# The rotary part of the row maxima as pairs of 64-row products on the two halves of TensorE

## The chip, the cores and the metric

The kernel runs on one core of a Trainium2 chip. The metric is the device time of one execution in microseconds, as the median of several runs. A profile of one execution stands beside it: what each engine did, instruction by instruction. The engines are TensorE (PE in the profile, with its weight loads as PEld), VectorE (DVE), ScalarE (ACT), GpSimd (POOL) and SyncE (SP), which issues transfers.

## The reference

Two layers of a diffusion backbone over 1024 latent tokens and 256 context tokens, 1024 channels wide. Layer 0 is multi-head latent attention with eight heads, layer 1 a gated long convolution. The change lies in the attention of layer 0. A query and a key have a part of 128 channels that each head has for itself and a rotary part of 64 channels, of which the key's is shared by all heads:

```python
def scores(qn_, qr_, kn_, kr_):
    s = jnp.einsum('bqhd,bkhd->bhqk', qn_, kn_) + jnp.einsum('bqhr,bkr->bhqk', qr_, kr_)
    return s.astype(jnp.float32) * scale
...
s = jnp.concatenate([scores(qn_b, qr_b, kn, kr), scores(qn_b, qr_b, knc, krc)], axis=-1)
p = jax.nn.softmax(s, axis=-1).astype(v.dtype)
```

The latent queries read 1024 + 256 = 1280 keys.

## The kernel before, in words

Everything is float32. For exactness a value is split into a high part, rounded to the narrower fp32r, and the rest, also fp32r; `split` (L95) makes the first by a cast on ACT and the second by a subtraction on DVE. A product of two split values is three matmuls (`mm3`, L117, its matmuls on L119 to L121): high with high, high with low, low with high.

The program has three stages: the projections of layer 0 and the filters of layer 1 (to about 435 us in the profile), the attention (to about 910 us), and layer 1. In the attention the work is cut into 16 units, each one head and 512 queries (`units`). For each unit `attend` goes over ten blocks of 128 keys: five matmuls make the transposed scores S (three with the split keys `kn` and queries `qn`, one of `krh` with `r1` at L825, one of `krl` with `r2` at L826), ACT takes the exponential, ACT and DVE split it, DVE adds it to `acc`, and three matmuls add its product with the values to O. At the end of a unit DVE takes the reciprocal of the sums (L855).

The rotary parts lie in tiles made for these five matmuls. `krh` has the high part of the key's 64 channels twice, in rows 0 to 63 and again in 64 to 127. `r1` has the high part of the queries' 64 channels in one half and the low part in the other, so that one matmul over 128 rows gives the key's high part times both. `r2` has the high part in rows 0 to 63, for the key's low part in `krl`, and in row 64 the negative row maximum, which a row of ones in `krl` subtracts from the scores. `rope` makes `r1` and `r2` for two heads at a time (L745 to L751).

The row maxima are what `row_max` (L755) makes for the unit ahead. For each of four tiles of 128 queries and each of three key segments (512, 512 and 256 wide, `ksegs`) it takes one of the two buffers of the PSUM pool `apx`, puts into it the product of the high parts `qn[0]` and `kn[0]` (L762) and that of `r1` and `krh` (L763, over 128 rows), and DVE reduces it to its maximum (L764). That is 12 buffers a unit, 192 in all. Each maximum is moved by a matmul with an identity (L769) and negated into row 64 of `r2`. The maxima only shift the exponent and cancel in the softmax.

`row_max` is a generator that yields after each buffer. `advance` lets it go two steps for each block of the unit that is being attended to. A scheduler then puts each engine's instructions into one fixed order; engines run theirs in that order and wait for each other by semaphores. Elsewhere the kernel has other matmuls that use a part of TensorE's array: `packed` (L123 to L134, matmul at L128) puts four products on 32 columns each, for the modulation vectors and the sums of squares, and `rms_steps` transposes pieces of 128, 96 or 64 rows at L396.

Of the kernel before, what the change touches and what calls it, by code (L numbers as in the profile page):

```python
# [11 lines left out]
F32 = mybir.dt.float32  # L12
F32R = mybir.dt.float32r
AF = mybir.ActivationFunctionType
ALU = mybir.AluOpType
AX = mybir.AxisListType
# [3 lines left out]
P = 128  # L20
# [35 lines left out]
class Net:  # L56
# [627 lines left out]
    def attention(self):  # L684
        nc, a = self.nc, self.a
        v, act, mm = nc.vector, nc.scalar, nc.tensor.matmul
        ps = self.open("psA", 2, space=PSUM)
        bank = lambda: ps.tile([P, 512], F32, tag="pj", name="pj")
        px = self.open("psX", 2, space=PSUM)
        tp = self.open("attt", 2)  # L690
        ckv, krh, krl, cq, cos, sin = self.att
# [5 lines left out]
        ksegs = [(0, 512), (512, 512), (1024, 256)]  # L697
# [33 lines left out]
        def rope(wb, sl):  # L731
            b = bank()
            for k in range(KQ):
                c = slice(P * k, P * k + P)
                self.mm3(b, (wb[0][:, c], wb[1][:, c]), (cq[0][k][:, sl], cq[1][k][:, sl]), k == 0, k == KQ - 1)
            x, y, q = [tp.tile([P, 512], F32, tag=f"rp{i}", name="rp", bufs=1) for i in range(3)]
            act.copy(out=x, in_=b)
            for p in range(0, P, 32):
                nc.sync.dma_start(out=y[p ^ 32 : (p ^ 32) + 32], in_=x[p : p + 32])
            v.tensor_tensor(out=q, in0=x, in1=cos[:, sl], op=ALU.mult)  # L740
            yield
            v.tensor_tensor(out=y, in0=y, in1=sin[:, sl], op=ALU.mult)
            v.tensor_tensor(out=q, in0=q, in1=y, op=ALU.add)
            out = []
            for j in range(2):  # L745
                r1 = tp.tile([P, 512], F32R, tag="r1", name="r1", bufs=5)
                r2 = tp.tile([65, 512], F32R, tag="r2", name="r2", bufs=5)
                me, ot = slice(64 * j, 64 * j + 64), slice(64 - 64 * j, 128 - 64 * j)
                act.copy(out=r1[me], in_=q[me])
                v.tensor_tensor(out=r1[ot], in0=q[me], in1=r1[me], op=ALU.subtract)  # L750
                act.copy(out=r2[0:64], in_=r1[me])  # L751
                out.append((r1, r2))
            return out

        def row_max(kn, qn, r1, r2):  # L755
            cm = tp.tile([P, 4, 3], F32, tag="cm", name="cm")
            mx = tp.tile([P, 4], F32R, tag="mx", name="mx")
            for t in range(4):
                c = slice(P * t, P * t + P)
                for i, (o, w) in enumerate(ksegs):  # L760
                    b = px.tile([P, 512], F32, tag="apx", name="apx")
                    mm(b[:, :w], lhsT=qn[0][:, c], rhs=kn[0][:, o : o + w], start=True, stop=False)  # L762
                    mm(b[:, :w], lhsT=r1[:, c], rhs=krh[:, o : o + w], start=False, stop=True)  # L763
                    v.tensor_reduce(out=cm[:, t, i : i + 1], in_=b[:, :w], axis=AX.X, op=ALU.max)  # L764
                    yield
            v.tensor_reduce(out=mx, in_=cm, axis=AX.X, op=ALU.max)
            b = bank()
            for t in range(4):
                mm(b[0:1, P * t : P * t + P], lhsT=mx[:, t : t + 1], rhs=identr, start=True, stop=True)  # L769
            act.activation(out=r2[64:65], in_=b[0:1], func=AF.Copy, scale=-1.0)  # L770
# [6 lines left out]
        def ahead():  # L777

            for pr in range(HEADS // 2):
                wc = self.kvw if pr == 0 else self.load_kv_weights(pr)  # L780
                wq, wr = self.qw if pr == 0 else self.load_q_weights(pr)
                vals[pr] = (wc, [])
                rr = {}
                for j in range(2):
                    kn = yield from keys(wc, j)
                    for sl in halves:
                        if j == 0:
                            rr[sl.start] = yield from rope(wr, sl)
                        qn = queries(wq, j, sl)
                        yield  # L790
                        if not ready and pr == 0 and len(vals[0][1]) == 0:
                            vals[0][1].extend(value(wc, t) for t in range(10))
                        r1, r2 = rr[sl.start][j]
                        yield from row_max(kn, qn, r1, r2)
                        ready[pr, j, sl.start] = (kn, qn, r1, r2)
# [652 lines left out]
```

## Time and profile before

| What | Value |
|---|---|
| Median of three runs | 1736.26 us (1733.69 to 1740.81) |
| The profiled execution's own time | 1731.71 us |
| Span from its first to its last instruction | 1729.9 us |
| Mean granted clock of TensorE over the span | 0.979 |
| Span before the attention stage, of it and after it, roughly | 435, 475 and 820 us |
| Reductions of the row maxima on DVE | 192, from 446.9 to 908.9 us |

A line of a group in the profile reads: source line, engine, operation, tile written and tiles read, shapes, count, then the busy time in us and the mean of one in ns, then the idle time of the engine just before and what ended it. A line of the timeline reads: start, duration (both us), engine, source line, operation. For a matmul `64*128` means 64 contraction rows and 128 columns of the array. Matmuls are pipelined: each is shown from its start to the modelled end of its last result, so neighbours overlap, and the cost of one in a row of them is the distance between starts.

### The profile page before, as it was taken

How to read it: one execution, taken by the hardware profiler on the slowest of the kernel's cores; microseconds unless marked ns; L12 is line 12 of the kernel's file. 1: busy time of each engine (PE TensorE's matmuls, PEld its weight loads, DVE VectorE, ACT ScalarE, POOL GpSimd, SP SyncE). 2: the span in 40 equal slices, each digit the busy share in tenths (PEclk: the TensorE clock that was granted, in tenths of full speed). 3: DMA queues.
4: the chain of work that ended last, by engine and by line, in shares of the span. 5: the costliest groups of instructions: out<-in, count | busy, mean ns of one | idle time of the engine just before them, and what ended most of it. 6: DMA issues, size and time to landing. Idle time of an engine off the chain costs nothing.

```text
span 1729.9 us, 22940 instructions
## 1 busy us (share of the span) xinstructions
PE 1633.5 (94%) x8160; PEld 1299.5 (75%) x8160; DVE 1442.2 (83%) x2558; ACT 766.3 (44%) x1337; POOL 16.0 (1%) x43
## 2 busy tenths in 40 slices
PE   5899897899999999999999999999999999999996
PEld 2467676787788788788787777888888888887874
DVE  4886979895699899899899456999999999999856
ACT  4533444445455465555555345433433433343313
POOL 1000000000000000000000010000000000000000
PEclk9899999899999999999999999999999999999998
DMA  9777664436101001010014771332332332244545
GB/s 342 256 231 222 200 187 120 138 89 206 28 27 37 25 32 38 19 33 25 25 56 132 232 254 64 101 98 83 101 115 83 104 106 89 95 122 134 180 142 197
DMA packets 140759, 206.15 MB, mean 119 GB/s; under 512 B 13578, under 2 KB 71649, under 8 KB 140516
## 3 DMA queue, kind: packets, MB, share of 16 engines
q1 hardware_dynamic: 137508, 194.00, 35.7%
q0 software_dynamic: 3136, 10.69, 1.9%
q8 instruction: 64, 1.05, 0.3%
q14 instruction: 51, 0.42, 0.1%
HBM read 148.92 MB, written 53.61 MB: 117 GB/s over the span
## 4 chain that ended last, share of the span: by engine, by line
PE 75%; DVE 10%; DMA 9%; ACT 3%; issue 2%; SPq 1%; DVEq 0%; ACTq 0%
PE pj L121 12%; PE pj L119 12%; PE pj L120 12%; DMA dec<-in_dec 2%; PE O L120 2%; PE S L119 2%; PE O L119 2%; PE S L826 2%; PE O L121 2%; PE apx L762 2%; PE S L825 2%; PE S L121 2%; PE S L120 2%; PE apx L763 2%; PE fu L119 2%; PE fy L119 2%
## 5 line engine op out<-in xcount | busy, mean ns | idle before, releaser
L96 ACT CAST w<-wr 128x512 fp32r<-128x512 f32 (+1 forms) x149 | 90.7, 609 | 259.5 <-PE pj L120 129.5
L119 PE MATMUL pj<-a,w 128*128 128x512 f32 x512 | 203.1, 397 | 1.7 <-ACT a L422 1.6
L121 PE MATMUL pj<-a,w 128*128 128x512 f32 x512 | 203.1, 398 | 0.0
L120 PE MATMUL pj<-a,w 128*128 128x512 f32 x512 | 203.0, 397 | 0.0
L828 ACT ACTIVATE p<-S 128x512 f32<-128x512 f32 x160 | 95.7, 598 | 148.2 <-DVE acc L835 69.5
L97 DVE TENSOR_TENSOR w<-wr,w 128x512 fp32r<-128x512 f32 (+1 forms) x149 | 98.8, 671 | 54.7 <-ACT w L96 54.6
L96 ACT CAST bh<-raw 128x512 fp32r<-128x512 f32 x128 | 77.1, 620 | 89.1 <-DVE raw L1071 71.0
L119 PEld LDWEIGHTS pj<-a,w 128*128 128x128 f32 x512 | 96.4, 188 | 22.0 <-ACT a L422 2.4
L120 PEld LDWEIGHTS pj<-a,w 128*128 128x128 f32 x512 | 96.5, 188 | 19.9 <-DVE a L423 0.2
L121 PEld LDWEIGHTS pj<-a,w 128*128 128x128 f32 x512 | 96.6, 189 | 19.5 <-issue 0.8
L97 DVE TENSOR_TENSOR p<-p 128x512 fp32r<-128x512 f32 x160 | 109.4, 684 | 1.5 <-ACT p L96 1.2
L764 DVE TENSOR_REDUCE cm<-apx 128x1 f32<-128x512 f32 (+1 forms) x192 | 107.1, 591 | 3.8 <-PE apx L763 3.1
L835 DVE TENSOR_TENSOR acc<-acc,p 128x512 f32<-128x512 f32 x144 | 98.7, 685 | 7.6 <-ACT p L828 6.7
L121 PE MATMUL pj<-pg,w 128*128 128x512 f32 (+1 forms) x248 | 96.5, 389 | 8.7 <-DVE w L97 8.6
L96 ACT CAST p<-p 128x512 fp32r<-128x512 f32 x160 | 99.5, 622 | 4.8
L119 PE MATMUL pj<-pg,w 128*128 128x512 f32 (+1 forms) x248 | 95.7, 389 | 2.7 <-ACT pg L422 2.7
L120 PE MATMUL pj<-pg,w 128*128 128x512 f32 (+1 forms) x248 | 96.6, 389 | 0.6 <-DVE pg L423 0.6
L97 DVE TENSOR_TENSOR bl<-raw,bh 128x512 fp32r<-128x512 f32 x128 | 84.7, 686 | 9.1 <-ACT bh L96 9.0
L119 PE MATMUL u<-bh,fm 128*128 128x256 f32 (+1 forms) x200 | 68.2, 342 | 12.2 <-ACT bh L96 9.5
L762 PE MATMUL apx<-kn,qn 128*128 128x512 f32 (+1 forms) x192 | 69.0, 364 | 2.2 <-DVE cm L764 1.9
L321 DVE TENSOR_TENSOR kk<-ph,dec 128x512 f32<-128x512 f32 x64 | 42.6, 684 | 33.2 <-DMA dec<-in_dec 26.6
L763 PE MATMUL apx<-krh,r 128*128 128x512 f32 (+1 forms) x192 | 67.1, 357 | 0.0
(312 smaller groups left out, 4408.9 us busy)
## 6 DMA issues: line engine op xcount, KB each, us to landing
aw<-in_adaw SPq DMA_DIRECT2D x32, 512.0 KB
kd<-ko SPq DMA_DIRECT2D x128, 128.0 KB
wr<-in_hw SPq DMA_DIRECT2D x64, 256.0 KB
kt<-kd SPq DMA_DIRECT2D x56, 256.0 KB
wr<-in_w SPq DMA_DIRECT2D x34, 256.0 KB
dec<-in_dec SPq DMA_DIRECT2D x64, 128.0 KB
pg<-in_adaw SPq DMA_DIRECT2D x32, 256.0 KB
wr<-in_wo SPq DMA_DIRECT2D x32, 256.0 KB
```

Of the source, the lines that this page charges most:

```text
L96: self.nc.scalar.copy(out=hi, in_=raw)
L97: self.nc.vector.tensor_tensor(out=lo, in0=raw, in1=hi, op=ALU.subtract)
L119: mm(out, lhsT=w[0], rhs=x[0], start=start, stop=False)
L120: mm(out, lhsT=w[0], rhs=x[1], start=False, stop=False)
L121: self.last = mm(out, lhsT=w[1], rhs=x[0], start=False, stop=stop)
L321: nc.vector.tensor_tensor(out=kk, in0=ps, in1=dec.broadcast_to([P, 2, 2, P]), op=ALU.mult)
L762: mm(b[:, :w], lhsT=qn[0][:, c], rhs=kn[0][:, o : o + w], start=True, stop=False)
L763: mm(b[:, :w], lhsT=r1[:, c], rhs=krh[:, o : o + w], start=False, stop=True)
L764: v.tensor_reduce(out=cm[:, t, i : i + 1], in_=b[:, :w], axis=AX.X, op=ALU.max)
L825: mm(S, lhsT=krh[:, c], rhs=r1, start=False, stop=False)
L828: act.activation(out=p, in_=S, func=AF.Exp, scale=ASCALE)
L835: v.tensor_tensor(out=acc, in0=acc, in1=p, op=ALU.add)
```

## The change

The changed kernel takes the rotary product of a buffer with the queries' high part alone, which has 64 rows. Two buffers are taken together. The first has its rotary product on rows 0 to 63 of TensorE (the high part in `r2`, the first copy in `krh`), the second on rows 64 to 127 (the high part in `r1`, the second copy in `krh`), each with a tile position that names its half. The one on the upper rows is issued first, the other right behind it. The low part of the queries is left out of the maxima. The six pairs of a unit are the two 512-wide segments of each query tile, and the 256-wide segments of two query tiles; the products with `kn` stay one for each buffer, and so do the reductions, which now stand behind the pair. `rope` puts the high part for both heads into rows 64 to 127 of `r1`, with the same number of casts, subtractions and copies.

```diff
-                me, ot = slice(64 * j, 64 * j + 64), slice(64 - 64 * j, 128 - 64 * j)
-                act.copy(out=r1[me], in_=q[me])
-                v.tensor_tensor(out=r1[ot], in0=q[me], in1=r1[me], op=ALU.subtract)
-                act.copy(out=r2[0:64], in_=r1[me])
+                me = slice(64 * j, 64 * j + 64)
+                same = r2[0:64] if j == 0 else r1[64:128]
+                act.copy(out=same, in_=q[me])
+                v.tensor_tensor(out=r1[0:64], in0=q[me], in1=same, op=ALU.subtract)
+                act.copy(out=r1[64:128] if j == 0 else r2[0:64], in_=same)
...
-            for t in range(4):
-                c = slice(P * t, P * t + P)
-                for i, (o, w) in enumerate(ksegs):
-                    b = px.tile([P, 512], F32, tag="apx", name="apx")
-                    mm(b[:, :w], lhsT=qn[0][:, c], rhs=kn[0][:, o : o + w], start=True, stop=False)
-                    mm(b[:, :w], lhsT=r1[:, c], rhs=krh[:, o : o + w], start=False, stop=True)
-                    v.tensor_reduce(out=cm[:, t, i : i + 1], in_=b[:, :w], axis=AX.X, op=ALU.max)
-                    yield
+            for pair in (((0, 0), (0, 1)), ((0, 2), (1, 2)), ((1, 0), (1, 1)),
+                         ((2, 0), (2, 1)), ((2, 2), (3, 2)), ((3, 0), (3, 1))):
+                halves_ = []
+                for half, (t, i) in enumerate(pair):
+                    o, w = ksegs[i]
+                    c = slice(P * t, P * t + P)
+                    b = px.tile([P, 512], F32, tag="apx", name="apx")[:, :w]
+                    mm(b, lhsT=qn[0][:, c], rhs=kn[0][:, o : o + w], start=True, stop=False)
+                    rows, rq = slice(64 * half, 64 * half + 64), (r2, r1)[half]
+                    halves_.append((b, rq[rows, c], krh[rows, o : o + w], (64 * half, 0)))
+                    if half == 0:
+                        yield
+                (b0, w0, k0, p0), (b1, w1, k1, p1) = halves_
+                prev = mm(b1, lhsT=w1, rhs=k1, start=False, stop=True, tile_position=p1)
+                with self.tc.issue_after(prev.ins), self.tc.high_priority():
+                    mm(b0, lhsT=w0, rhs=k0, start=False, stop=True, tile_position=p0)
+                for (t, i), h in zip(pair, halves_):
+                    v.tensor_reduce(out=cm[:, t, i : i + 1], in_=h[0], axis=AX.X, op=ALU.max)
+                yield
```

The order of the instructions moves with it. On PE, in the middle of a unit, two buffers of the maxima (a 512-wide and a 256-wide one) stood before as follows; S and O are the unit being attended to, `r_5972` is `r1` of the unit ahead and `r_5623` that of the present one:

```order
L762 MATMUL apx<-kn,qn 128x512
L763 MATMUL apx<-krh,r_5972 128x512
L121 MATMUL S<-qn,kn 128x512
L762 MATMUL apx<-kn,qn 128x256
L763 MATMUL apx<-krh,r_5972 128x256
L825 MATMUL S<-r_5623,krh 128x512
L826 MATMUL S<-r_5624,krl 128x512
```

Near the same place it now reads (L766 is the product with `kn`, L772 the upper half, L774 the lower half from `r2`, here `r_5973`):

```order
L766 MATMUL apx<-kn,qn 128x256
L120 MATMUL S<-qn,kn 128x512
L121 MATMUL S<-qn,kn 128x512
L766 MATMUL apx<-kn,qn 128x256
L772 MATMUL apx<-krh,r_5972 128x256
L774 MATMUL apx<-krh,r_5973 128x256
L837 MATMUL S<-r_5623,krh 128x512
```

Each buffer had its rotary product right behind its first product; now the first buffer stays open over other matmuls until the second has its own first product, and the two rotary products stand side by side between full ones.

In the first unit, before which there is no unit to attend to, the last three buffers stood before as follows on PE, with the transposing product of the maxima behind them:

```order
L763 MATMUL apx<-krh,r_4518 128x512
L762 MATMUL apx<-kn,qn 128x512
L763 MATMUL apx<-krh,r_4518 128x512
L762 MATMUL apx<-kn,qn 128x256
L763 MATMUL apx<-krh,r_4518 128x256
L769 MATMUL pj<-identr,mx 1x128 x4
```

The last six buffers now read:

```order
L766 MATMUL apx<-kn,qn 128x512 x2
L772 MATMUL apx<-krh,r_4518 128x512
L774 MATMUL apx<-krh,r_4519 128x512
L766 MATMUL apx<-kn,qn 128x256 x2
L772 MATMUL apx<-krh,r_4518 128x256
L774 MATMUL apx<-krh,r_4519 128x256
L766 MATMUL apx<-kn,qn 128x512 x2
L772 MATMUL apx<-krh,r_4518 128x512
L774 MATMUL apx<-krh,r_4519 128x512
L781 MATMUL pj<-identr,mx 1x128 x4
```

Two first products now stand together ahead of each pair, with nothing else between one pair and the next.

## The prediction

> **What bounds the kernel now.** I read the page first, for the engine that carries the end. Its lines on busy time and on the chain that ended last:
>
> ```profile
> PE 1633.5 (94%) x8160; PEld 1299.5 (75%) x8160; DVE 1442.2 (83%) x2558; ACT 766.3 (44%) x1337; POOL 16.0 (1%) x43
> ...
> PE 75%; DVE 10%; DMA 9%; ACT 3%; issue 2%; SPq 1%; DVEq 0%; ACTq 0%
> ```
>
> TensorE carries three quarters of the chain. The rows that the change touches all lie in the attention stage, so next comes the table by windows for 435 to 910 us (columns: length, busy time and count of PE, PEld, DVE, ACT, POOL, then the granted clock) and, of the waits between 460 and 908 us, those that TensorE's weight loads had:
>
> ```profile
> 435.00:910.00 475.00, 471.06 (x2241) 380.23 (x2241) 418.69 (x684) 259.02 (x456) 0.00 (x0) 1.00 0.10 30
> ```
>
> ```profile
> PEld S L119 <- ACT p L828: 3.6, 7, 0.8
> PEld apx L762 <- DVE cm L764: 2.9, 7, 0.6
> PEld apx L762 <- ACT qn L96: 2.1, 11, 0.2
> ```
>
> PE is busy 471.06 of 475 us at full clock, and its longest kind of wait sums to 3.6 us. DVE is next, at 418.69 us, 88%. So what TensorE gains or loses here goes almost whole to the end, as long as DVE's 56 us of air are not used up.
>
> What one matmul costs is read from starts, because a busy matmul overlaps the next. The timeline of PE, a steady piece (start, duration, instruction), and the weight loads beside it:
>
> ```profile
> 599.76 0.40 PE L763 MATMUL apx<-krh,r 128*128 128x512 f32 x1
> 599.99 0.39 PE L121 MATMUL S<-qn,kn 128*128 128x512 f32 x1
> 600.22 0.28 PE L762 MATMUL apx<-kn,qn 128*128 128x256 f32 x1
> 600.33 0.28 PE L763 MATMUL apx<-krh,r 128*128 128x256 f32 x1
> 600.45 0.39 PE L825 MATMUL S<-r,krh 128*128 128x512 f32 x1
> ```
>
> ```profile
> 600.22 0.19 PEld L763 LDWEIGHTS apx<-krh,r 128*128 128x128 f32 x1
> 600.34 0.19 PEld L825 LDWEIGHTS S<-r,krh 128*128 128x128 f32 x1
> ```
>
> A 512-wide matmul takes 0.23 us to the next start, a 256-wide one 0.12. The next one starts about 0.16 us before the modelled end (599.99 + 0.39 = 600.38 against 600.22), and each weight load (L763's at 600.22) starts while the matmul before is under way (L762, 600.22), one place ahead of its own (600.33). That hiding is what the change puts at risk.
>
> **The change part by part: what it removes.** The rotary products are these groups (by shape: line, engine, tile, count, busy time and mean ns), and the reductions behind them:
>
> ```profile
> L763 PE MATMUL apx<-krh,r 128*128 128x512 f32 x128 | 49.4, 396 | 0.0
> ...
> L763 PE MATMUL apx<-krh,r 128*128 128x256 f32 x64 | 18.0, 281 | 0.0
> ```
>
> ```profile
> L764 DVE TENSOR_REDUCE cm<-apx 128x1 f32<-128x512 f32 x128 | 83.8, 678 | 3.2 <-PE apx L763 2.9
> ...
> L764 DVE TENSOR_REDUCE cm<-apx 128x1 f32<-128x256 f32 x64 | 26.6, 416 | 0.6 <-PE apx L763 0.2
> ```
>
> They become 64 pairs of 512 and 32 pairs of 256. If the two of a pair stream side by side, a pair takes the place of one product: 64 x 0.23 + 32 x 0.12 = 14.7 + 3.8 = 18.6 us saved on PE, at most. The reductions stay 192, of the same sizes.
>
> **What it adds: 96 excursions into a half-array arrangement.** No row here shows two 64-row products side by side, so the price comes from the nearest rows: the transposes of L396 that contract 64 rows, amid full matmuls (PE, then the weight loads):
>
> ```profile
> 181.68 0.28 PE L121 MATMUL u<-bh,fm 128*128 128x256 f32 x1
> 181.80 0.45 PE L119 MATMUL u<-bh,fm 128*128 128x512 f32 x1
> 182.18 0.46 PE L396 MATMUL pj<-ident,st 64*128 64x64 f32 x4
> 182.56 0.39 PE L318 MATMUL ph<-fw,hf 128*128 128x256 f32 x1
> 182.79 0.28 PE L319 MATMUL ph<-fw,hf 128*128 128x256 f32 x1
> ```
>
> ```profile
> 182.18 0.32 PEld L396 LDWEIGHTS pj<-ident,st 64*128 64x128 f32 x4 [0.24 <-issue]
> 182.56 0.19 PEld L318 LDWEIGHTS ph<-fw,hf 128*128 128x128 f32 x1
> 182.67 0.19 PEld L319 LDWEIGHTS ph<-fw,hf 128*128 128x128 f32 x1
> ```
>
> Three things differ from the steady piece. The transposes start 0.07 us before the modelled end ahead of them (181.80 + 0.45 = 182.25), not 0.16: 0.09 lost going in. L318 does the same (182.18 + 0.46 = 182.64 against 182.56): 0.08 to 0.09 lost coming out. And the loads no longer run ahead: those of L396 and L318 stand at the starts of their own matmuls, so L318 takes 0.23 to the next start where a 256-wide one takes 0.12: 0.11 lost. That it is the 64 rows, and not that they are transposes, the same line with 96 rows shows; its loads start ahead:
>
> ```profile
> 391.47 0.28 PE L121 MATMUL u<-bh,fm 128*128 128x256 f32 x1
> 391.59 0.33 PE L396 MATMUL pj<-ident,st 96*128 96x96 f32 x2
> ```
>
> ```profile
> 391.48 0.25 PEld L396 LDWEIGHTS pj<-ident,st 96*128 96x128 f32 x2
> ```
>
> The kernel's other excursion, the products on a quarter of the columns at L128, has the same signature:
>
> ```profile
> 1000.44 0.40 PE L120 MATMUL pj<-og,w 128*128 128x512 f32 x1
> 1000.68 0.40 PE L121 MATMUL pj<-og,w 128*128 128x512 f32 x1
> 1001.00 1.06 PE L128 MATMUL nb<-sq,ones 128*32 128x512 f32 x8
> 1002.00 0.50 PE L119 MATMUL pj<-og,w 128*128 128x512 f32 x1
> 1002.34 0.39 PE L120 MATMUL pj<-og,w 128*128 128x512 f32 x1
> 1002.57 0.39 PE L121 MATMUL pj<-og,w 128*128 128x512 f32 x1
> ```
>
> ```profile
> L128 PE MATMUL nb<-sq,ones 128*32 128x512 f32 x32 | 4.3, 605 | 1.9 <-ACT sq L380 1.9
> ```
>
> In: 0.32 to the next start instead of 0.23; out: 0.34 instead of 0.23. So I price an excursion at 0.09 in, 0.11 for the pair's first load in the open, 0.09 out and 0.11 for the load behind it: 0.40 us, for a pair that saves 0.23 or 0.12. The Trainium skill, TensorEngine Tiling (Array Packing), Key Properties, says that a change of tiling mode, not merely of tile, drains TensorE; these rows agree, with 0.09 us on each crossing, while the loads in the open are not in that sentence.
>
> For a 512-wide pair that is 0.40 + 0.23 = 0.63 against 0.46 before, +0.17; for a 256-wide one 0.40 + 0.12 = 0.52 against 0.24, +0.28. Sum: 64 x 0.17 + 32 x 0.28 = 10.9 + 9.0 = **+19.9 us**, on an engine with no air. Per pair the ends are -0.23 (no loss at either crossing, loads hidden) and, with the halves one after the other and the second load in the open too, 0.40 + 0.11 = +0.51.
>
> The Trainium skill, TensorE: Matmul & The Clock Gate, Part 3, states a pack's span as one matmul plus about 4 ns per further tile, and 3.07 times for four row tiles; by that alone the 96 pairs would give the 18.6 us, and no run here shows it. I follow the rows.
>
> **The two buffers of apx.** Before, a product's buffer was reduced while the other was filled. Now both are held until the pair is done, and the next pair's first product, two matmuls later in its own order, waits for a reduction of 0.68 us. In the steady units the scheduled order puts four or more other matmuls (4 x 0.23 us) in between for all but five pairs, and DVE has 12% of air; but a reciprocal holds DVE for long once per unit:
>
> ```profile
> L855 DVE RECIPROCAL acc<-pj 128x512 f32<-128x512 f32 x16 | 53.6, 3350 | 0.0
> ```
>
> Nothing to a reduction per pair (64 x 0.68 + 32 x 0.42 = 57 us) are the ends; nearest is the wait that already exists, 2.9 us. I take +2. In the first unit nothing lies between; there DVE's rows of before are:
>
> ```profile
> 451.82 1.01 DVE L764 TENSOR_REDUCE cm<-apx 128x1 f32<-128x512 f32 x2
> 453.32 1.71 DVE L764 TENSOR_REDUCE cm<-apx 128x1 f32<-128x512 f32 x3 [0.49 <-PE apx L763]
> 455.44 1.71 DVE L764 TENSOR_REDUCE cm<-apx 128x1 f32<-128x512 f32 x3 [0.41 <-PE apx L763]
> 457.18 0.17 DVE L766 TENSOR_REDUCE mx<-cm 128x4 fp32r<-128x12 f32 x1
> ```
>
> The last eight reductions take 5.4 us. Now they are four pairs, 3 x 1.36 + 0.83 = 4.9 us of reducing, with three gaps in which one plain product, the crossing and the pair run: 0.23 + 0.09 + 0.11 + 0.23 + some 0.2 of tail, 0.85 each. That is 7.5 us, **+2**.
>
> **Without a price.** The rounding of q makes as many casts, subtractions and copies, of the same 64x512, in another order, on ACT (259 of 475 us busy) and DVE; both have air that covers a changed order; without it a 512-wide pass of some 0.68 us for each of the 8 rope calls would stand in the open, 5 us. DMAs are unchanged.
>
> **Sum.** The profiled execution took 1731.7 us (span 1729.9); +19.9 + 2 + 2 = +24 gives **1756 us**. The runs of before have a median of 1736.3, 4.5 us above the profiled one; the same sum there gives 1760, and the range has to hold both.
>
> **Rivals.**
> - *The crossing is free and loads run ahead* (the faster side). Place: L772 and L774 between two full products. For it: the halves use different rows, and the crossings seen here are of transposes and columns. Against it: the 64-row transposes. It decides if the crossings and loads of a pair cost under 0.19 us together. Then -18.6 + 4 for the buffers: 1717 us. Chance 0.08.
> - *The array drains, but the loads run ahead.* 0.18 a pair: 64 x (0.41 - 0.46) + 32 x (0.30 - 0.24) = -1.3 us, +4: 1734 us. Against it: the load of L318 at 182.56, in the open. Chance 0.10.
> - *The halves do not share the array, or their loads do not.* One load more in the open, 96 x 0.11 = 10.6: 1766 us; products one after the other, 18.6: 1774 us. For it: no row shows two row halves together. Against it: the products of L128, eight of them in 1.00 us where one has a mean of 605 ns: four column strips do run side by side. Chance 0.14.
> - *DVE's queue holds both buffers of apx*, 0.2 us more for each pair: 96 x 0.2 = 19: 1775 us. Against it: DVE's air, and the matmuls between. Chance 0.08.
> - The forecast, pairs that cross at some 0.40 us: chance 0.60.
>
> **Numbers.** The range runs from 1734 (drain with hidden loads) to 1776 (a buffer wait or serial halves); outside lie the faster rival and the worst of the slow ones. About 0.5%, 8.7 us, is what a measurement of this kernel can tell from no change. Slower by more: 0.60 + 0.14 + 0.08 = 0.82, less 0.02 for a forecast that comes out small: 0.80. Within: 0.10 + 0.02 = 0.12. Faster: 0.08.
>
> **What would show it.** In the profile after, L772's starts should be 0.32 after a 512-wide matmul, with L772's load at its own start and not ahead; L774 some 0.01 after L772; the next full matmul about 0.43 later and its successor 0.34 later. PE's busy time in the stage should grow by about 20 us with the count of matmuls the same. I am wrong if the loads of L772 or of the matmul behind L774 stand ahead of the crossing, if L774 starts 0.1 or 0.23 after L772, or if waits for cm at L766 sum to over 10 us.

## The result

| | Before | Changed | Ratio (95% interval) |
|---|---|---|---|
| Median of the runs side by side | 1736.89 us (4 runs) | 1752.95 us (4 runs) | 1.0096 (1.0074 to 1.0118) |
| A second measurement of the same two | 1736.81 us (7 runs) | 1752.80 us (4 runs) | 1.0089 (1.0067 to 1.0111) |
| Profiled execution, span | 1729.9 us | 1749.0 us | |

The change makes the kernel slower by 16 us, 0.9%. The forecast was 24 us.

The page of the changed kernel, busy time:

```profile
PE 1654.4 (95%) x8160; PEld 1287.2 (74%) x8160; DVE 1443.1 (83%) x2558; ACT 764.2 (44%) x1337; POOL 16.5 (1%) x43
```

Each engine has as many instructions as before. Only TensorE is busier by more than a microsecond (20.9 us), while its weight loads are busy 12 us less, though as many are issued. Here is one excursion into the 64-row arrangement in the timeline of PE, and the weight loads beside it:

```profile
488.70 0.39 PE L119 MATMUL S<-qn,kn 128*128 128x512 f32 x1
488.93 0.40 PE L766 MATMUL apx<-kn,qn 128*128 128x512 f32 x1
489.26 0.49 PE L772 MATMUL apx<-krh,r 64*128 64x512 f32 x1
489.26 0.49 PE L774 MATMUL apx<-krh,r 64*128 64x512 f32 x1
489.69 0.50 PE L120 MATMUL S<-qn,kn 128*128 128x512 f32 x1
490.03 0.40 PE L121 MATMUL S<-qn,kn 128*128 128x512 f32 x1
```

```profile
488.71 0.19 PEld L766 LDWEIGHTS apx<-kn,qn 128*128 128x128 f32 x1
489.26 0.18 PEld L772 LDWEIGHTS apx<-krh,r 64*128 64x128 f32 x1 [0.36 <-issue]
489.26 0.18 PEld L774 LDWEIGHTS apx<-krh,r 64*128 64x128 f32 x1
489.69 0.19 PEld L120 LDWEIGHTS S<-qn,kn 128*128 128x128 f32 x1 [0.24 <-issue]
489.79 0.19 PEld L121 LDWEIGHTS S<-qn,kn 128*128 128x128 f32 x1
```

L774 starts in the same hundredth of a microsecond as L772, and so do their loads: the two halves load and stream side by side. What the pair loses is around it. From L766 to L772 are 0.33 us where an undisturbed 512-wide matmul has 0.23; from L774 to the next full matmul 0.43; from that to its successor 0.34. The loads of L772, L774 and L120 stand at the starts of their own matmuls, and the record names no semaphore that they wait for ("issue"); L121's load, inside the full arrangement again, is ahead of its matmul. All 96 pairs stand so in the trace, and the means of the groups by shape show the open load (a load that does not run ahead of its matmul) in the durations: 500 and 386 ns where the full products before had 396 and 281.

```profile
L772 PE MATMUL apx<-krh,r 64*128 64x512 f32 x64 | 32.0, 500 | 0.0
L774 PE MATMUL apx<-krh,r 64*128 64x512 f32 x64 | 31.8, 498 | 0.0
...
L774 PE MATMUL apx<-krh,r 64*128 64x256 f32 x32 | 12.4, 386 | 0.0
L772 PE MATMUL apx<-krh,r 64*128 64x256 f32 x32 | 12.4, 386 | 0.0
```

### The profile page after: what moved, and what is told of

Read it like the earlier page. It is cut to its first block, busy times and chain, and to the rows that moved or that the text cites. A ratio compares the mean times of both kernels' runs of the same rounds, so it can differ in the third digit from the quotient of the medians.

```text
span 1749.0 us, 22939 instructions
## 1 busy us (share of the span) xinstructions
PE 1654.4 (95%) x8160; PEld 1287.2 (74%) x8160; DVE 1443.1 (83%) x2558; ACT 764.2 (44%) x1337; POOL 16.5 (1%) x43
## 4 chain that ended last, share of the span: by engine, by line
PE 77%; DVE 9%; DMA 8%; ACT 3%; issue 2%; SPq 1%; DVEq 0%; ACTq 0%
PE pj L121 12%; PE pj L119 12%; PE pj L120 12%; PE O L120 2%; PE apx L766 2%; PE apx L772 2%; PE O L119 2%; PE S L119 2%; PE S L837 2%; PE O L121 2%; PE S L121 2%; PE S L120 2%; PE fu L119 2%; PE S L838 2%; PE fy L119 2%; DMA aw<-in_adaw 2%
## 5 line engine op out<-in xcount | busy, mean ns | idle before, releaser
L120 PE MATMUL pj<-a,w 128*128 128x512 f32 x512 | 203.1, 397 | 0.0
L121 PE MATMUL pj<-a,w 128*128 128x512 f32 x512 | 203.0, 398 | 0.0
L776 DVE TENSOR_REDUCE cm<-apx 128x1 f32<-128x512 f32 (+1 forms) x192 | 105.9, 592 | 21.9 <-PE apx L774 17.1
L120 PEld LDWEIGHTS pj<-a,w 128*128 128x128 f32 x512 | 96.5, 188 | 19.8 <-DVE a L423 0.3
L121 PEld LDWEIGHTS pj<-a,w 128*128 128x128 f32 x512 | 96.6, 189 | 19.5 <-issue 0.8
L121 PE MATMUL pj<-pg,w 128*128 128x512 f32 (+1 forms) x248 | 98.5, 397 | 8.4 <-DVE w L97 8.4
L119 PE MATMUL pj<-pg,w 128*128 128x512 f32 (+1 forms) x248 | 97.1, 395 | 2.3 <-ACT pg L422 2.3
L120 PE MATMUL pj<-pg,w 128*128 128x512 f32 (+1 forms) x248 | 98.0, 395 | 0.6 <-DVE pg L423 0.6
L766 PE MATMUL apx<-kn,qn 128*128 128x512 f32 (+1 forms) x192 | 66.7, 364 | 2.3 <-DVE cm L776 2.2
L120 PE MATMUL u<-bl,fm 128*128 128x256 f32 (+1 forms) x200 | 66.3, 333 | 0.5 <-DVE bl L97 0.2
```

What stands on the lines that cost most here:

```text
L119: mm(out, lhsT=w[0], rhs=x[0], start=start, stop=False)
L120: mm(out, lhsT=w[0], rhs=x[1], start=False, stop=False)
L121: self.last = mm(out, lhsT=w[1], rhs=x[0], start=False, stop=stop)
L766: mm(b, lhsT=qn[0][:, c], rhs=kn[0][:, o : o + w], start=True, stop=False)
L776: v.tensor_reduce(out=cm[:, t, i : i + 1], in_=h[0], axis=AX.X, op=ALU.max)
```

## The experiments

Three theories stood against each other. A: each excursion into the 64-row arrangement costs TensorE some 0.40 us, and inside it the halves run side by side. B: the two held buffers of `apx` and the later reductions cost the time. C: 64-row products are slow or serial in themselves. Each run was compared with runs of the kernel before on the same chip. The edits are shown against the changed kernel, but for the single products, whose edit is made to the kernel before.

### The pairs' order with full products

```diff
-                    halves_.append((b, rq[rows, c], krh[rows, o : o + w], (64 * half, 0)))
+                    halves_.append((b, r1[:, c], krh[:, o : o + w], (0, 0)))
...
-                prev = mm(b1, lhsT=w1, rhs=k1, start=False, stop=True, tile_position=p1)
+                prev = mm(b1, lhsT=w1, rhs=k1, start=False, stop=True)
...
-                    mm(b0, lhsT=w0, rhs=k0, start=False, stop=True, tile_position=p0)
+                    mm(b0, lhsT=w0, rhs=k0, start=False, stop=True)
```

> The changed kernel's order with both buffers of apx held until the pair is done, but each rotary product over all 128 rows of r1 and krh, with no tile position; the maxima have the low part again. Theory A (each excursion into 64 rows costs some 0.40 us of TensorE, the halves stream side by side): the crossings go, the streams come back, so the steady units take what they took before and only the first unit stays longer, by 2 to 4 us: 1737 to 1742 us. Theory B (the loss comes from holding both buffers and from the late reductions): the loss stays, 1753 us or more. Theory C (a 64-row product is slow in itself, or the halves run one after the other, with no fixed cost of a crossing): as A, 1737 to 1742.

Measured: 1737.31 us against 1734.70, ratio 1.0008 (0.9993 to 1.0023). The orders on DVE and ACT are those of the changed kernel, and on PE all but 19 of 8160 places are. So B falls: holding both buffers, reducing late and filling `r1` and `r2` in another order cost together at most 4 us, and no difference from before is resolved. The bulk of the loss is in the 64-row form.

### Single products of 64 rows

```diff
-                    mm(b[:, :w], lhsT=r1[:, c], rhs=krh[:, o : o + w], start=False, stop=True)
+                    mm(b[:, :w], lhsT=r2[0:64, c], rhs=krh[0:64, o : o + w], start=False, stop=True)
```

> The order of the kernel before, each buffer for itself, but the rotary product takes the 64 rows of the high part alone (r2 and krh, rows 0 to 63), with no tile position: 192 excursions of one product each; the low part is left out of the maxima. Theory A: 192 x 0.40 = 77 us more than before, about 1814 us, if 64 rows alone make the excursion, as the 64-row transposes showed. Theory B: the buffers are as before, about 1737 us. Theory C: a slow 64-row product without a fixed crossing, which has to explain 16 us for 192 products, gives 1745 to 1757.

Measured: 1802.99 us against 1734.70, ratio 1.0395 (1.0375 to 1.0415), 68 us more. The timeline of PE in this kernel shows the excursion of a single product, with no tile position named:

```profile
540.28 0.40 PE L762 MATMUL apx<-kn,qn 128*128 128x512 f32 x1
540.61 0.50 PE L763 MATMUL apx<-krh,r 64*128 64x512 f32 x1
541.04 0.50 PE L120 MATMUL S<-qn,kn 128*128 128x512 f32 x1
541.38 0.40 PE L121 MATMUL S<-qn,kn 128*128 128x512 f32 x1
541.61 0.40 PE L825 MATMUL S<-r,krh 128*128 128x512 f32 x1
541.85 0.40 PE L826 MATMUL S<-r,krl 65*128 65x512 f32 x1
542.09 0.39 PE L119 MATMUL O<-p,v 128*128 128x512 f32 x1
```

0.33, 0.43 and 0.34 again, the same with one product as with two. The 65-row product of L826 has 0.24 on both sides: it is not an excursion. So the 64 rows are enough, and the cost is one of the crossing. A is right on the mechanism; 77 us were expected and 68 came, of which more below. Eight of the 192 products stand right behind another one, so that there are 184 excursions (73 us at 0.40). In these eight, on the same half, the second product adds a stream of its own: from the first at 480.27 us to the next full matmul at 480.94, for instance, are 0.67 us and not 0.43, where two products on different halves start 3 ns apart. C, which allowed 1757 at most, falls as far as a slow product without a crossing goes.

### Two pairs in one excursion

```diff
+        zeror = tp.tile([P, P], F32R, name="zeror", bufs=1)
+        act.activation(out=zeror, in_=self.ident, func=AF.Copy, scale=0.0)
...
-                prev = mm(b1, lhsT=w1, rhs=k1, start=False, stop=True, tile_position=p1)
-                with self.tc.issue_after(prev.ins), self.tc.high_priority():
-                    mm(b0, lhsT=w0, rhs=k0, start=False, stop=True, tile_position=p0)
+                prev = mm(b1, lhsT=w1, rhs=k1, start=False, stop=False, tile_position=p1)
+                for bb, ww, kk, pp, end in ((b0, w0, k0, p0, False), (b1, zeror[64:128], k1, p1, True),
+                                            (b0, zeror[0:64], k0, p0, True)):
+                    with self.tc.issue_after(prev.ins), self.tc.high_priority():
+                        prev = mm(bb, lhsT=ww, rhs=kk, start=False, stop=end, tile_position=pp)
```

> The changed kernel with a second pair right behind the first in the same excursion, on the same halves, with weights of zero: the same maxima, twice the 64-row products, the same 96 excursions. Theory A: only the stream of one more product per pair is added, 64 x 0.23 + 32 x 0.12 = 18.6 us: about 1772 us, with the added pair 0.23 or 0.12 behind the first. Theory B: TensorE is not what sets the time, about 1753. Theory C: the whole time of a pair comes again, 64 x 0.63 + 32 x 0.52 = 57 us: about 1810.

Measured: 1770.71 us against 1734.70, ratio 1.0207 (1.0175 to 1.0239): 36 us over before, so some 20 over the changed kernel. The timeline of PE:

```profile
499.63 0.39 PE L768 MATMUL apx<-kn,qn 128*128 128x512 f32 x1
499.95 0.49 PE L774 MATMUL apx<-krh,r 64*128 64x512 f32 x1
499.95 0.49 PE L778 MATMUL apx<-krh,r 64*128 64x512 f32 x1
500.28 0.39 PE L778 MATMUL apx<-krh,zeror 64*128 64x512 f32 x2
500.60 0.50 PE L121 MATMUL O<-p,v 128*128 128x512 f32 x1
```

From L774 at 499.95 to the next full matmul at 500.60 are 0.65 us, where one pair has 0.43: the second pair adds 0.22, a single stream, its loads hidden (duration 0.39). It starts 0.33 and not 0.23 behind the first, because the first pair's open load lies in that distance. This is A's 18.6 us, not C's 57.

### The first unit without pairs

```diff
-        def row_max(kn, qn, r1, r2):
+        def row_max(kn, qn, r1, r2, first):
...
+            for t in range(4 if first else 0):
+                c = slice(P * t, P * t + P)
+                for i, (o, w) in enumerate(ksegs):
+                    b = px.tile([P, 512], F32, tag="apx", name="apx")
+                    mm(b[:, :w], lhsT=qn[0][:, c], rhs=kn[0][:, o : o + w], start=True, stop=False)
+                    mm(b[:, :w], lhsT=r1[:, c], rhs=krh[:, o : o + w], start=False, stop=True)
+                    v.tensor_reduce(out=cm[:, t, i : i + 1], in_=b[:, :w], axis=AX.X, op=ALU.max)
+                    yield
+            for pair in () if first else (((0, 0), (0, 1)), ((0, 2), (1, 2)), ((1, 0), (1, 1)),
...
```

> The changed kernel, but the first unit's row maxima in the form of before: single buffers and full 128-row products; the other 15 units keep their pairs. By theory A with the first unit's chain of pairs and reductions, which the two traces put at 3.7 us longer, about 1749 us; the 90 excursions that are left keep the rest of the loss. If the first unit's added time is chance, 1752 to 1753. If the first unit carried the loss, about 1738.

Measured: 1745.71 us against 1734.70, ratio 1.0068 (1.0047 to 1.0090). Against the changed kernel's 1.0096 and 1.0089 that is 4 to 5 us less, close to the 3.7 expected, though the intervals overlap. DVE's last reductions of the first unit, in the changed kernel:

```profile
457.43 1.29 DVE L776 TENSOR_REDUCE cm<-apx 128x1 f32<-128x512 f32 x2 [0.36 <-PE apx L774]
459.73 1.29 DVE L776 TENSOR_REDUCE cm<-apx 128x1 f32<-128x512 f32 x2 [1.02 <-PE apx L774]
462.20 0.76 DVE L776 TENSOR_REDUCE cm<-apx 128x1 f32<-128x256 f32 x2 [1.18 <-PE apx L774]
464.67 1.29 DVE L776 TENSOR_REDUCE cm<-apx 128x1 f32<-128x512 f32 x2 [1.71 <-PE apx L774]
465.99 0.17 DVE L778 TENSOR_REDUCE mx<-cm 128x4 fp32r<-128x12 f32 x1
```

The last eight take 465.99 - 457.43 = 8.6 us instead of 5.4, with DVE idle ahead of each pair until its L774 ends. The same rows of the kernel with the pairs' order and full products:

```profile
460.51 1.29 DVE L776 TENSOR_REDUCE cm<-apx 128x1 f32<-128x512 f32 x2 [0.24 <-PE apx L772]
462.62 1.29 DVE L776 TENSOR_REDUCE cm<-apx 128x1 f32<-128x512 f32 x2 [0.82 <-PE apx L772]
464.50 0.76 DVE L776 TENSOR_REDUCE cm<-apx 128x1 f32<-128x256 f32 x2 [0.59 <-PE apx L772]
466.08 1.29 DVE L776 TENSOR_REDUCE cm<-apx 128x1 f32<-128x512 f32 x2 [0.82 <-PE apx L772]
467.40 0.17 DVE L778 TENSOR_REDUCE mx<-cm 128x4 fp32r<-128x12 f32 x1
```

Here they take 6.9 us: of the 3.2 us that the first unit loses, 1.5 come from the held buffers, which this kernel has too, and 1.7 come on top of that in the changed kernel. Of these 1.7, the first of the three gaps between the pairs gives 0.20 us (1.02 against 0.82). The other two give 0.59 and 0.89, and there TensorE's clock had fallen to half, as shown further down; the two causes are not separated.

### Fewer excursions for the same products

Four buffers of `apx` were made (S has two banks instead of three, `pj` one instead of two), so that four 512-wide products could share an excursion; the 256-wide ones became full and single. The control holds the buffers in the same way and has full products throughout. The core of the edit with 64-row products against the changed kernel comes first, and behind the last dots the main line in which the control (+) differs from it (-):

```diff
+            for four in ((0, 1), (2, 3)):
...
+                for n in (1, 0, 3, 2):
+                    b, wt, k, pos = got[n]
...
+                        prev = mm(b, lhsT=wt, rhs=k, start=False, stop=True, tile_position=pos)
...
-                        got.append((b, rq[rows, c], krh[rows, o : o + w], (64 * half, 0)))
+                        got.append((b, r1[:, c], krh[:, o : o + w]))
```

> Control for the next run: four buffers of apx (one bank less for S and one less for pj, since PSUM has eight), the 512-wide segments of two query tiles taken as four buffers that are held together, their rotary products full ones over 128 rows; the 256-wide ones each for itself, full. No excursion at all. All theories: the price of the fewer banks for S and pj alone, 1735 to 1760 us.

Measured: 1760.99 us against 1736.81, ratio 1.0134 (1.0114 to 1.0153).

> The run before this with the four rotary products as two pairs of 64-row halves in one excursion, 32 excursions in all. Theory A (a fixed cost for each excursion): one takes 0.40 + 2 x 0.23 = 0.86 us against 4 x 0.23 = 0.92, so the time is that of the control less 2 us, within 4 us of it either way. Theory C (the cost comes with each pair, not with each excursion): 64 x 0.17 = 11 us more than the control.

Measured: 1765.92 us, ratio 1.0162 (1.0140 to 1.0183). That is 4.9 us over the control, with intervals that overlap, between the two expectations (2 us less and 11 more), and as set up the run does not tell A from C. The timeline says why. It is PE's, of two groups of four of one unit:

```profile
491.50 0.73 PE L778 MATMUL apx<-krh,r 64*128 64x512 f32 x4
492.16 0.50 PE L849 MATMUL S<-r,krh 128*128 128x512 f32 x1
```

```profile
496.24 0.49 PE L778 MATMUL apx<-krh,r 64*128 64x512 f32 x2
496.67 0.49 PE L766 MATMUL apx<-kn,qn 128*128 128x512 f32 x1
497.09 0.50 PE L778 MATMUL apx<-krh,r 64*128 64x512 f32 x2
497.53 0.50 PE L120 MATMUL O<-p,v 128*128 128x512 f32 x1
```

The first group crosses once, and its four products and the way out take 0.66 us where a pair has 0.43; the scheduler split the second and put a full product into it, so that it crosses twice. Over the trace that is 16 excursions of four and 32 of two, 48 and not 32. By A's prices 48 x 0.40 - 64 x 0.23 = 19.2 - 14.7 = +4.5 us, which is what came; but this was worked out afterwards. No version beat the kernel before: the fewer banks and the four held buffers, which no run separates, cost 24 us without any excursion.

### The changed kernel again

> The changed kernel as it is, beside the next two on one chip, for a closer ratio. Theory A: crossings of 0.40 us against streams saved add 19.5 us on TensorE; the other runs say that some 6 us of that went into waits that TensorE had anyway, and that the first unit's chain adds 2 to 4 us: 13 to 17 us more than before, 0.8% to 1.0%.

Measured: 1752.80 us, ratio 1.0089 (1.0067 to 1.0111), 16 us, as expected.

## Why the prediction was right, and where it was off

**The price of an excursion** was right to the hundredth of a microsecond. In the changed kernel's trace the median start-to-start distances of the 64 wide pairs are 326 ns into L772, 3 ns from it to L774, 424 to the next full matmul and 337 to its successor; forecast were 0.32, 0.01, 0.43 and 0.34. The 64-row transposes and the column products of the trace before were good stand-ins for a pair of halves, of which that trace had none.

**That the halves share the array** was right (3 ns apart). The rival of serial halves or serial loads falls, and the rival with free crossings falls with the rows of L772, L120 and their loads. The span rule of the Trainium skill (TensorE: Matmul & The Clock Gate, Part 3) holds inside the excursion, with 3 ns where it gives about 4 for a further tile; it says nothing of the way in and out, which here costs more than the pair gains.

**The drain with loads that run ahead** falls too: L772's load stands at 489.26, with its own matmul. The rival in which DVE's queue holds both buffers falls with the pairs' order and full products. In the changed kernel's trace the waits for `cm` at L766 sum to 2.3 us between 460 and 930 us, and all of them lie in the first unit.

**"On an engine with no air" was the step that failed in size.** The windows below run from the first unit's L769 (L781, L789 in the others) to the last product with the values, in the kernel before, the one with pairs but for the first unit, and the one with full products in the pairs' order. In the kernel before that end lies at 945 us; at about 910, which was named as the end of the attention, only the row maxima end.

```profile
457.40:945.20 487.80, 485.14 (x2273) 390.76 (x2274) 436.95 (x704) 274.86 (x479) 0.00 (x0) 1.00 0.12 37
```

```profile
463.22:963.17 499.95, 499.21 (x2274) 374.55 (x2274) 437.37 (x704) 272.93 (x479) 0.00 (x0) 1.00 0.11 36
```

```profile
467.62:955.96 488.34, 486.41 (x2274) 391.14 (x2275) 435.96 (x703) 273.12 (x479) 0.00 (x0) 1.00 0.12 37
```

90 pairs add 12.1 us. By the forecast's prices they are 60 x 0.17 + 30 x 0.28 = 18.6. I took every start-to-start distance of these windows apart, into 231, 118 or 60 ns by width, 93 ns for each crossing, 105 ns for each open load, and the rest as waiting. Before: 475.5 us of streams and 12.3 of waiting. With 90 pairs: 458.4 of streams, 35.6 of crossings and open loads (0.396 each), and 5.9 of waiting. So the streams gave back 17.1 (forecast: 60 x 0.23 + 30 x 0.12 = 17.4), the excursions took 35.6, and 6.4 us of the bill were paid out of waits that TensorE had anyway for exponentials, reductions and splits. The forecast took TensorE to have no air, from the page's busy time (471 of 475 us) and the longest kind of wait, 3.6 us. But neighbours overlap by 0.16 us in these records, so that a matmul that begins 0.05 late leaves no idle time and shows in neither. The same holds in the other traces, the stretch of halved clock described below left aside: 6.1 us of waiting in the changed kernel, 6.4 in its second profile, 6.2 with two pairs in an excursion, and 5.0 with the single products, where 73 us by the count of excursions became 68. With full products in the pairs' order, where nothing had to be absorbed, it is 11.5.

**The buffers of apx.** The +2 for the steady units was too much: with the pairs' order and full products this window has 488.34 us against 487.80, and some of that is halved clock. The +2 for the first unit was too little: 3.2 us, and more behind it. The granted clock (before the DMA share in each row) in windows of 6 us, in the changed kernel:

```profile
456.00:462.00 6.00, 4.19 (x15) 1.92 (x13) 3.42 (x7) 0.37 (x1) 0.00 (x0) 0.89 0.00 0
462.00:468.00 6.00, 3.90 (x14) 2.36 (x13) 2.21 (x5) 0.58 (x1) 0.00 (x0) 0.50 0.00 0
468.00:474.00 6.00, 6.00 (x22) 4.67 (x21) 1.26 (x3) 3.17 (x5) 0.00 (x0) 0.76 0.13 31
```

In the chain of pairs TensorE worked two thirds of the time and its clock was halved, until some 5 us into the next unit, where TensorE is busy throughout. The kernel before has 1.00 in the windows at this place, and the one with the first unit unchanged too. But the 64-row form is not needed for it: with the pairs' order and full products the clock falls as well, if for 3.4 us and not for 10.2:

```profile
462.00:468.00 6.00, 3.48 (x15) 1.99 (x16) 3.50 (x7) 0.00 (x0) 0.00 (x0) 0.92 0.00 0
468.00:474.00 6.00, 6.00 (x23) 4.71 (x21) 0.69 (x1) 3.08 (x5) 0.00 (x0) 0.79 0.07 17
```

In the kernel with single 64-row products it falls for 10.2 us too (0.82, 0.50 and 0.83 in its windows from 456 us on), without any held buffers. With the part of the halved clock behind L781, the changed kernel's window from there on is 2.1 us over the 499.95 above:

```profile
466.21:968.25 502.04, 501.28 (x2274) 376.17 (x2275) 437.42 (x704) 273.20 (x479) 0.00 (x0) 1.00 0.11 36
```

**The sum.** First unit 3.2, the 90 pairs 12.1, the halved clock 2.1: 17.4 us. With 0.5 that the first unit loses ahead of its last eight reductions, this is the 18.0 us by which the stretch from the first product into S (at 440.4 us before, 445.4 in the changed kernel) to the last product with the values is longer in the profile. The two spans differ by 19.1, because the work ahead of that stretch took 5.1 us more and the work behind it 3.9 less; two profiles of the changed kernel differ by 3.3 us at its start. The medians differ by 16. The first unit and the halved clock together are 5.8 us by the traces, where the run without pairs in the first unit gave 4 to 5.

Forecast were 19.9 + 2 + 2. Against the 18.0 of the profile, it had 6.4 us of absorbed waits and the 2 for the steady units too much. It had 2.1 too little for the halved clock, for which there was no term, and 0.5 too little for the first unit: 3.2 with the price of its six pairs (of which four stand in the sum twice, as excursions and in the gaps), against 3.7. That these cancel in part is luck. That the absorbed waits are the largest part of the difference rests on the accounting of the traces above; no run changed the waits alone. Why the clock fell in these stretches and not in those of the two kernels with the first unit of before stays open.

## What to carry to other kernels

A product that contracts 64 rows amid full ones pays for a change of arrangement, here 0.40 us for each excursion, whether it holds one product, two side by side or four; so count excursions, not products, and use the halves only where several pairs can stand together, which needs the PSUM buffers and an order that keeps them together. Here no version with 64-row products gained time. A small price of this kind can often be read beforehand from unrelated instructions of the same trace, such as transposes of 64 rows, by the distance between starts and by whether the weight load stands ahead. And an engine that is busy 99% of a stage by its records can still have some per cent of waiting in the distances between starts (12.3 of 488 us here), which takes up part of a loss. That it would swallow part of a gain likewise was not tried.

## What was not expected of the hardware

A 64-row contraction with no tile position named crosses like one with a named half (0.33, 0.43, 0.34 us in the single products), while 65 rows do not (0.24). And the granted clock fell to half, at 460.7 us, in a stretch where TensorE was still busy 4.19 and 3.90 of 6 us. Its longest idle time ahead of the fall was 0.77 us, and 1.58 us within the stretch:

```profile
460.48 0.44 PE L766 MATMUL apx<-kn,qn 128*128 128x256 f32 x1 [0.77 <-DVE cm L776]
...
462.69 1.22 PE L766 MATMUL apx<-kn,qn 128*128 128x512 f32 x2 [0.52 <-DVE cm L776]
463.83 0.79 PE L772 MATMUL apx<-krh,r 64*128 64x512 f32 x1
463.84 0.79 PE L774 MATMUL apx<-krh,r 64*128 64x512 f32 x1
466.21 0.59 PE L781 MATMUL pj<-identr,mx 128*1 128x128 f32 x4 [1.58 <-DVE mx L778]
```

Each product of the pair takes 0.79 us here instead of 0.49. The kernel before, busy 4.76 and 5.10 of 6 us in the windows of its first unit, kept its clock:

```profile
450.00:456.00 6.00, 4.76 (x22) 2.92 (x20) 4.65 (x10) 0.64 (x2) 0.00 (x0) 1.00 0.00 0
456.00:462.00 6.00, 5.10 (x25) 4.14 (x26) 2.00 (x5) 2.59 (x4) 0.00 (x0) 1.00 0.05 12
```

The Trainium skill, TensorE: Matmul & The Clock Gate, Part 1, gives idle windows of about 3.4 us as what halves the clock; no pause of that length stands in these rows, so here less than that was enough. What does decide is not shown: the share of time in which TensorE is busy by its records does not. With single 64-row products it was busy 3.16 of the 3.40 us ahead of the fall, while the kernel before kept its clock over a stretch with 2.40 of 3.41.
